# A squared-ReLU transformer block on one core: another order for the first four blocks, the last pair of blocks and the last token tiles

## Chip, core and metric

The kernel runs on one core of one Trainium2 chip. Its time is the device time of one execution in microseconds (us); of several runs the median is given. The engines are named as the profile names them: PE (TensorE, matmul), PEld (its weight loads), DVE (VectorE), ACT (ScalarE), POOL (GpSimd) and SP (SyncE, which issues loads and stores here). Each engine works through its own instructions in the order in which the program lists them.

## What is computed

One layer on a sequence of 1024 tokens with 1024 features: a mixer, then an MLP. Only the MLP is touched:

```python
h = rms_norm(x, norm2_pre) * (1.0 + scale2) + shift2
f = jnp.square(jax.nn.relu(h @ w_fc1)) @ w_fc2      # 1024 -> 4096 -> 1024
x = x + gate2 * rms_norm(f, norm2_post)
```

## The kernel before

Every fp32 product is made of three passes: each operand is split into a high part (a cast by ACT) and a low part (a subtraction by DVE), and PE multiplies high by high, low by high and high by low.

**First product of the MLP, `expand()`.** Both matrices are cut into quarters, and seven products of sums of quarters (a Strassen scheme, numbered 1 to 7) take the place of eight. The 4096 columns of `w_fc1` are worked in 16 blocks n = 0 to 15 (`FP`). A product m of block n is `run(m, n)`: 12 matmuls (4 k-steps by 3 passes) of 128x512. Products 1, 6, 5 and 3 of a block add up in one PSUM bank (`alpha`, tiles a0 to a15), products 7 and 4 in a second (`pi`, p0 to p15), product 2 in a third (`beta`, b0 to b15). After some of them the running sum has to be taken out of the bank before the next product adds to it; that is `after(m, n)`: a copy by ACT after 1, 7 and 6, an add by DVE after 2, 4 and 5, and after 3 a copy, a Relu and a Square by ACT. A block's results lie in a tile F with three parts, and the pool of F tiles (`hx`) has two buffers, so block n takes the buffer of block n - 2 when that has been read. `block_sums(n)` is four DVE instructions that make five sums (tiles S and S3, one buffer each) out of F and c11 (the result of products 1 and 2), stored to DRAM by POOL; c11 of the first four blocks has by then been stored and is loaded again (`again(n)`, tiles c11r). The weights of a block come as two tiles (wa, wo); `T1`, `T32`, `T4` are DVE subtractions that make sums of their quarters, `hi_of` and `lo_of` make the high and low parts that PE reads (hia and loa for products 1 and 2, hic and loc for 7 and 6, hib and lob for 4 and 5; `b22` and `b22_lo` make bhi and blo for product 3).

For the first four blocks all these calls are written out by hand, line by line (lines 882 to 1031), since the token side of the second half is made ready at the same time; from block 4 on a loop repeats one pattern (lines 1032 to 1078). Blocks 2 and 3 run side by side, with products 1 and 2 of block 4 between their last ones. In the loop a block's products come as 7, 6, 4, then 1 of the next block, 5, then 2 of the next block, 3. The last block has no next one, so its five products 7, 6, 4, 5, 3 follow each other, with the calls that make ready the first steps of the next product (`second.fill`).

**Second product, `contract()`.** Seven products again (order 5, 3, 7, 4, 2, 1, 6), each 8 steps of 24 matmuls over four token tiles. In the last product the last two steps are done tile by tile, so that a tile is complete after its 12 last matmuls and goes through `done(6, i, ...)`: `more_of` (DVE adds the bank to acc), `weigh` (ACT squares and sums, DVE updates the mean square and hands it to POOL's power function, DVE multiplies by the gate G), and `finish` (two DVE instructions that scale and add the residual, and two stores on SP). `finish` needs POOL's result.

Of the kernel before, what the change touches and what calls it, by code (L numbers as in the profile page):

```python
# [8 lines left out]
F32 = mybir.dt.float32  # L9
# [7 lines left out]
P = 128  # L17
# [23 lines left out]
def block_kernel(  # L41
# [6 lines left out]
    nc = tc.nc  # L48
# [3 lines left out]
    NT = HT // P  # L52
# [532 lines left out]
    def load_a(n):  # L585
        wa[n] = load_cols(2 * n * P, f"wa{n}")

    def load_o(n):
        wo[n] = load_cols((2 * n + 1) * P, f"wo{n}")
# [6 lines left out]
    def hi_of(kind, n):  # L596
        src = {"a": wa, "c": wo, "b": wa}[kind][n]
        nc.scalar.copy(unit_tiles(kind, n)[0], src)  # L598

    def lo_of(kind, n):  # L600
        src = {"a": wa, "c": wo, "b": wa}[kind][n]
        hi, lo = unit[kind, n]
        nc.vector.tensor_tensor(lo, src, hi.bitcast(F32), ALU.subtract)  # L603

    def b22(n):
        unit["d", n] = (where[n // 2 % 2].tile([P, KH, P], F32R, tag="bhi", name=f"bhi{n}"),
                        where[n // 2 % 2].tile([P, KH, P], F32R, tag="blo", name=f"blo{n}"))
        nc.scalar.copy(unit["d", n][0], wo[n][:, KH:KT])

    def b22_lo(n):  # L610
        hi, lo = unit["d", n]
        nc.vector.tensor_tensor(lo, wo[n][:, KH:KT], hi.bitcast(F32), ALU.subtract)
# [5 lines left out]
    def T1(n):  # L618
        b11, b21, b12, b22 = parts(n)
        sub(b11, b12, b11)  # L620

    def T32(n):
        b11, b21, b12, b22 = parts(n)
        sub(b12, b22, b12)
        sub(b22, b22, b11)

    def T4(n):
        b11, b21, b12, b22 = parts(n)
        sub(b21, b21, b22)
# [96 lines left out]
    NF = 4  # L726
    FP = DFF // (2 * P)
# [4 lines left out]
    fD = [dram.tile([P, 2, 7, 512], F32, name=f"fD{kk}") for kk in range(FK)]  # L732
    F_A11, F_A22, F_S = 0, 1, 2
# [14 lines left out]
    def expand():  # L748
# [9 lines left out]
        hx = stage_pool("hx", 2)  # L758
# [73 lines left out]
        alpha, beta, pi, c11s, F = {}, {}, {}, {}, {}  # L832

        def run(m, n):
            bank = {2: beta, 4: pi, 7: pi}.get(m, alpha)
            if m in (1, 2, 7):
                bank[n] = ps_tile(f"{'abp'[(1, 2, 7).index(m)]}{n}")
            product(bank[n], m, n, m in (1, 2, 7))


        def after(m, n):
            if m == 1:
                c11s[n] = c11p.tile([P, 512], F32, tag="c11", name=f"c11_{n}")
                nc.scalar.copy(c11s[n], alpha[n])
            elif m == 2:
                c = add(c11s[n], beta[n], c11s[n])
                nc.vector.scalar_tensor_tensor(c, c, 0.0, c, ALU.max, ALU.mult)
                nc.gpsimd.dma_start(out=fD[n // 2][:, n % 2, F_A11], in_=c)
            elif m == 7:
                F[n] = hx.tile([P, 3, 512], F32, tag="F", name=f"F{n}")  # L850
                nc.scalar.copy(F[n][:, 0], pi[n])  # L851
            elif m == 6:
                nc.scalar.copy(F[n][:, 1], alpha[n])
            elif m == 4:
                add(F[n][:, 1], pi[n], F[n][:, 1])
            elif m == 5:
                add(F[n][:, 0], alpha[n], F[n][:, 0])
            else:
                nc.scalar.copy(F[n][:, 2], alpha[n])  # L859
                nc.scalar.activation(F[n], F[n], AF.Relu)  # L860
                nc.scalar.activation(F[n], F[n], AF.Square)  # L861
                nc.gpsimd.dma_start(out=fD[n // 2][:, n % 2, F_A22], in_=F[n][:, 0])

        def again(n):
            c11s[n] = c11p.tile([P, 512], F32, tag="c11", name=f"c11r_{n}")
            nc.sync.dma_start(out=c11s[n], in_=fD[n // 2][:, n % 2, F_A11])

        def block_sums(n):
            t, c = F[n], c11s[n]
            at = fD[n // 2][:, n % 2]  # L870
            s = late["fsum"].tile([P, 2, 512], F32, tag="S", name=f"S{n}")
            cb = c.rearrange("p (o n) -> p o n", o=1).broadcast_to([P, 2, 512])
            add(s, cb, t[:, 0:3:2])
            nc.gpsimd.dma_start(out=at[:, F_S:F_S + 2], in_=s)
            s = late["fsum"].tile([P, 3, 512], F32, tag="S3", name=f"S3_{n}")
            add(s[:, 0], t[:, 1], t[:, 0])
            sub(s[:, 1], t[:, 1], c)
            sub(s[:, 2], t[:, 2], t[:, 0])
            nc.gpsimd.dma_start(out=at[:, F_S + 2:], in_=s)
# [49 lines left out]
        T4(0)  # L929
        hi_of("b", 0)  # L930
        run(7, 0)
        after(2, 2)
        after(7, 0)
        his("A22")
        lo_of("b", 0)
# [3 lines left out]
        T4(1)  # L939
        hi_of("b", 1)  # L940
        run(6, 0)
        after(2, 3)
        after(6, 0)
        his("S1")
        lo_of("b", 1)
# [5 lines left out]
        again(0)  # L951
        load_a(3)
        load_o(3)
        again(1)
        run(4, 0)
        last_sums()
        after(4, 0)
# [12 lines left out]
        hi_of("c", 2)  # L970
        run(3, 0)
        after(5, 1)
        T1(3)
        b22_lo(3)
        lo_of("c", 2)
        T32(3)
        T4(2)
        run(3, 1)
        hi_of("c", 3)
        after(3, 0)  # L980
        hi_of("b", 2)
        lo_of("c", 3)
        after(3, 1)
        run(7, 2)
        block_sums(0)
        T4(3)
        lo_of("b", 2)
        after(7, 2)
        run(7, 3)
        hi_of("b", 3)  # L990
        load_a(4)
        run(6, 2)
        block_sums(1)
        lo_of("b", 3)
        after(6, 2)
        after(7, 3)
        again(2)
        load_o(4)
        load_a(5)
        run(6, 3)  # L1000
        hi_of("a", 4)
        after(6, 3)
        lo_of("a", 4)
        b22(4)
        run(4, 2)
        T1(4)
        run(5, 2)
        after(4, 2)
        b22_lo(4)
        run(4, 3)  # L1010
        after(5, 2)
        T32(4)
        hi_of("c", 4)
        run(3, 2)
        after(4, 3)
        T4(4)
        lo_of("c", 4)
        run(1, 4)
        after(3, 2)
        hi_of("b", 4)  # L1020
        run(5, 3)
        after(1, 4)
        again(3)
        lo_of("b", 4)
        hi_of("a", 5)
        run(2, 4)
        block_sums(2)
        after(5, 3)
        run(3, 3)
        lo_of("a", 5)  # L1030
        after(2, 4)
        for n in range(NF, FP):
            more = n + 1 < FP
            if more:
                load_o(n + 1)
                if n + 2 < FP:
                    load_a(n + 2)

            if more:
                b22(n + 1)  # L1040
            after(3, n - 1)
            if more:
                T1(n + 1)
                b22_lo(n + 1)
            else:
                second.fill(1)
            run(7, n)
            after(7, n)
            block_sums(n - 1)
            run(6, n)  # L1050
            after(6, n)
            if more:
                T32(n + 1)
                hi_of("c", n + 1)
            else:
                second.fill(2)
            run(4, n)
            after(4, n)
            if more:
                lo_of("c", n + 1)  # L1060
                T4(n + 1)
                hi_of("b", n + 1)
                run(1, n + 1)
                after(1, n + 1)
                lo_of("b", n + 1)
            run(5, n)
            after(5, n)
            if more:
                if n + 2 < FP:
                    hi_of("a", n + 2)  # L1070
                    lo_of("a", n + 2)
                run(2, n + 1)
                after(2, n + 1)
            else:
                second.fill(3)
            run(3, n)
        after(3, FP - 1)
        block_sums(FP - 1)
        st.close()
# [54 lines left out]
    def contract():  # L1134
# [44 lines left out]
        def more_of(c, i, ps, op=ALU.add):  # L1179
            nc.vector.tensor_tensor(at(c, i), at(c, i), ps, op)  # L1180

        def done(m, i, ps):
            if m == 5:
                put(11, i, ps, -1.0)
                put(12, i, ps)
            elif m == 3:
                put(22, i, ps)
                more_of(12, i, ps)
                weigh(i, 1, True)
            elif m == 7:  # L1190
                more_of(11, i, ps)
            elif m == 4:
                put(21, i, ps)
                more_of(11, i, ps)
            elif m == 2:
                more_of(21, i, ps)
                more_of(22, i, ps, ALU.subtract)
                weigh(NT + i, 0, True)
            elif m == 1:
                more_of(11, i, ps)  # L1200
                more_of(22, i, ps)
                weigh(i, 0, False)
                finish(i)
                fetch_x(NT + i, nc.gpsimd)
            else:
                more_of(22, i, ps)
                weigh(NT + i, 1, False)
                finish(NT + i)


        def gate_row(kt):
# [488 lines left out]
```

## Time and profile before

| | |
|---|---|
| median of 3 runs | 934.15 us (932.95 to 935.11) |
| the profiled execution's own time | 935.21 us |
| its span, first to last instruction | 933.5 us |
| PE busy | 892.4 us (96%), 3960 matmuls |
| DVE, ACT, POOL busy | 686.9 us (74%), 418.8 us (45%), 88.6 us (9%) |
| mean granted clock of TensorE | 0.989 of full speed |

A row of a timeline gives start and duration of an instruction in us, engine, line, operation and tiles, and in brackets the idle time of its engine just before it with what ended that. Matmuls overlap: each row lasts about 0.39 us, but they start some 0.23 us apart.

### The profile page before, as it was taken

The page shows a single profiled execution, that of the slowest core. Times are in us where ns is not written, and L with a number is a line of the kernel's source. Part 1 is how long each engine was busy: PE and PEld are TensorE (multiplying, and loading weights), DVE is VectorE, ACT ScalarE, POOL GpSimd, SP SyncE. Part 2 cuts the span into 40 slices and gives each one's busy share as a digit, 9 for nine tenths or more (in the row PEclk, how much of TensorE's full clock was granted, in tenths as well). Part 3 has the DMA queues.
Part 4 walks back from the last instruction along what each step waited for, and adds up shares of the span by engine and source line. Part 5 has one row for each costly group of instructions (what it writes and reads, how often), then busy time and mean ns, then how long its engine had stood idle before and what let it go on. Part 6 is the DMA issues. An engine that isn't in the chain of part 4 may idle for free.

```text
span 933.5 us, 10776 instructions
## 1 busy us (share of the span) xinstructions
PE 892.4 (96%) x3960; PEld 726.0 (78%) x3960; DVE 686.9 (74%) x980; ACT 418.8 (45%) x558; POOL 88.6 (9%) x147
## 2 busy tenths in 40 slices
PE   4999999999999997999999999999999999999993
PEld 3788678888887786788888888778888888888882
DVE  6889888799658984765666656567987774669694
ACT  3323674235367563445444354444445433434431
POOL 4001020012002000111110111100000000000032
PEclk9999999999999998999999999999999999999997
DMA  9934256575724336543444434489976884334753
GB/s 310 354 104 148 89 158 194 169 250 201 224 68 146 101 100 217 193 146 136 146 169 148 145 136 150 164 311 389 345 237 200 278 274 129 91 115 140 241 181 135
DMA packets 114105, 173.52 MB, mean 186 GB/s; under 512 B 6098, under 2 KB 61442, under 8 KB 114052
## 3 DMA queue, kind: packets, MB, share of 16 engines
q1 hardware_dynamic: 104292, 135.03, 45.0%
q0 software_dynamic: 9760, 37.80, 10.7%
q8 instruction: 31, 0.51, 0.2%
q14 instruction: 22, 0.18, 0.1%
HBM read 135.06 MB, written 37.75 MB: 185 GB/s over the span
## 4 chain that ended last, share of the span: by engine, by line
PE 49%; issue 34%; DVE 8%; ACT 4%; DMA 2%; POOL 1%; SPq 0%; POOLq 0%; DVEq 0%; ACTq 0%
PE a L828 5%; PE a L829 5%; PE a L830 5%; PE pb L1411 3%; PE p L828 2%; PE po L85 2%; PE p L830 2%; PE p L829 2%; PE pu L1586 2%; PE po L86 2%; PE po L87 2%; PE pv L85 2%; PE pv L87 2%; PE pv L86 2%; PE b L829 1%
## 5 line engine op out<-in xcount | busy, mean ns | idle before, releaser
L85 PE MATMUL m<-thi,shi 128*128 128x512 f32 x448 | 174.5, 390 | 0.0
L86 PE MATMUL m<-tlo,shi 128*128 128x512 f32 x448 | 174.5, 390 | 0.0
L87 PE MATMUL m<-thi,slo 128*128 128x512 f32 x448 | 174.5, 390 | 0.0
L94 DVE TENSOR_TENSOR slo<-s,shi 128x1024 fp32r<-128x1024 f32 x56 | 68.4, 1222 | 53.0 <-ACT shi L91 53.0
L91 ACT CAST shi<-s 128x1024 fp32r<-128x1024 f32 x56 | 58.9, 1052 | 102.7 <-PE m L86 61.2
L87 PEld LDWEIGHTS m<-thi,slo 128*128 128x128 f32 x448 | 84.2, 188 | 17.5
L86 PEld LDWEIGHTS m<-tlo,shi 128*128 128x128 f32 x448 | 84.2, 188 | 17.4
L85 PEld LDWEIGHTS m<-thi,shi 128*128 128x128 f32 x448 | 84.2, 188 | 17.3
L91 ACT CAST thi<-wt 128x1024 fp32r<-128x1024 f32 x40 | 42.1, 1052 | 42.1 <-DVE wt L571 34.5
L91 ACT CAST whi<-w_raw 128x1024 fp32r<-128x1024 f32 x28 | 29.3, 1052 | 52.6 <-DMA w_raw<-in_w_in_dram 15.2
L571 DVE TENSOR_TENSOR wt<-wt,b 128x1024 f32<-128x1024 f32 x32 | 39.1, 1222 | 17.4 <-DMA b<-in_w_fc_dram 15.8
L94 DVE TENSOR_TENSOR tlo<-wt,thi 128x1024 fp32r<-128x1024 f32 x40 | 48.9, 1223 | 2.2 <-ACT thi L91 0.8
L571 DVE TENSOR_TENSOR S<-c,F 128x1024 f32<-128x1024 f32 x12 | 14.7, 1225 | 42.4 <-ACT F L861 42.4
L94 DVE TENSOR_TENSOR wlo<-w_raw,whi 128x1024 fp32r<-128x1024 f32 x28 | 34.1, 1220 | 6.2 <-ACT whi L91 6.2
L859 ACT COPY F<-a 128x512 f32<-128x512 f32 x16 | 9.4, 585 | 59.4 <-PE a L830 59.4
L291 POOL TENSOR_TENSOR f<-msf,neg_half 128x1 f32<-128x1 f32 x8 | 7.2, 901 | 286.7 <-DVE msf L1153 286.7
L598 ACT CAST hic<-wo 128x1024 fp32r<-128x1024 f32 x16 | 16.8, 1052 | 35.3 <-DVE wo L571 35.3
L828 PE MATMUL p<-hA,hib 128*128 128x512 f32 x64 | 26.6, 416 | 5.9 <-ACT F L851 5.2
L603 DVE TENSOR_TENSOR lob<-wa,hib 128x1024 fp32r<-128x1024 f32 x16 | 19.6, 1224 | 16.9 <-ACT hib L598 16.9
L181 DVE SCALAR_TENSOR_TENSOR ada_acc<-ada_raw,silu_c,ada_acc 128x1024 f32<-128x1024 f32 x21 | 26.9, 1281 | 4.1 <-DMA ada_raw<-in_w_ada_dram 4.0
L598 ACT CAST hib<-wa 128x1024 fp32r<-128x1024 f32 x16 | 16.8, 1048 | 29.3 <-DVE wa L571 29.3
L828 PE MATMUL a<-hS,bhi 128*128 128x512 f32 x64 | 25.4, 397 | 2.7 <-DVE F L571 2.7
(311 smaller groups left out, 2200.1 us busy)
## 6 DMA issues: line engine op xcount, KB each, us to landing
s<-fD SPq DMA_DIRECT2D x56, 512.0 KB, 4.3
wt<-in_w_fc_dram SPq DMA_DIRECT2D x40, 512.0 KB, 5.2
ada_raw<-in_w_ada_dram SPq DMA_DIRECT2D x24, 512.0 KB, 4.5
fD<-S POOLq DMA_DIRECT2D x16, 768.0 KB, 4.0
wa<-in_w_fc_dram SPq DMA_DIRECT2D x20, 512.0 KB, 4.0
piece<-in_w_ada_dram SPq DMA_DIRECT2D x16, 512.0 KB, 8.3
w_raw<-in_w_out_dram SPq DMA_DIRECT2D x16, 512.0 KB, 4.4
wo<-in_w_fc_dram SPq DMA_DIRECT2D x16, 512.0 KB, 4.4
```

The costliest lines, as they stand in the source:

```text
L85: nc.tensor.matmul(ps, lhsT=ah, rhs=bh, start=start, stop=False)
L86: nc.tensor.matmul(ps, lhsT=ah, rhs=bl, start=False, stop=False)
L87: nc.tensor.matmul(ps, lhsT=al, rhs=bh, start=False, stop=stop)
L91: nc.scalar.copy(hi, src)
L94: nc.vector.tensor_tensor(lo, src, hi.bitcast(F32), ALU.subtract)
L181: nc.vector.scalar_tensor_tensor(acc, t, silu_c[:, kt:kt + 1], acc, ALU.mult, ALU.add)
L571: nc.vector.tensor_tensor(o, a, b, op)
L598: nc.scalar.copy(unit_tiles(kind, n)[0], src)
L828: nc.tensor.matmul(ps, lhsT=ah, rhs=bh, start=first, stop=False, skip_group_check=not start)
L829: nc.tensor.matmul(ps, lhsT=ah, rhs=bl, start=False, stop=False, skip_group_check=not start)
L830: nc.tensor.matmul(ps, lhsT=al, rhs=bh, start=False, stop=last, skip_group_check=not start)
L1411: nc.tensor.matmul(pbs[j], lhsT=w[:, j * P:(j + 1) * P], rhs=a, start=k == 0 and n == 0, stop=k == KT - 1 and n == 2)
```

## The change

The last call of `done` (line 1206 on): `finish` of a tile is called after the add of the following tile. The evictions `after(7, n)` and `after(6, n)` can come in either order; the store of F's first part becomes a function of its own, called by `block_sums` except for block 1. The calls of the first four blocks are written in another order, of which the diff shows the parts that the text speaks of. The last block is taken out of the loop and its products run as 6, 7, 5, 4, 3.

```diff
-            elif m == 7:
-                F[n] = hx.tile([P, 3, 512], F32, tag="F", name=f"F{n}")
-                nc.scalar.copy(F[n][:, 0], pi[n])
-            elif m == 6:
-                nc.scalar.copy(F[n][:, 1], alpha[n])
+            elif m in (6, 7):
+                if n not in F:
+                    F[n] = hx.tile([P, 3, 512], F32, tag="F", name=f"F{n}")
+                nc.scalar.copy(F[n][:, 7 - m], (alpha if m == 6 else pi)[n])
...
-                nc.gpsimd.dma_start(out=fD[n // 2][:, n % 2, F_A22], in_=F[n][:, 0])
+
+        def store_22(n):
+            nc.gpsimd.dma_start(out=fD[n // 2][:, n % 2, F_A22], in_=F[n][:, 0])
...
         def block_sums(n):
             t, c = F[n], c11s[n]
+            if n != 1:
+                store_22(n)
...
         run(7, 0)
-        after(2, 2)
         after(7, 0)
...
         hi_of("c", 2)
         run(3, 0)
         after(5, 1)
+        after(3, 0)
+        lo_of("c", 2)
         T1(3)
...
         run(3, 1)
         hi_of("c", 3)
-        after(3, 0)
         hi_of("b", 2)
+        after(3, 1)
+        block_sums(0)
         lo_of("c", 3)
-        after(3, 1)
+        lo_of("b", 2)
         run(7, 2)
-        block_sums(0)
+        load_a(4)
+        store_22(1)
+        after(7, 2)
+        after(2, 2)
...
-                second.fill(3)
             run(3, n)
+
+        n = FP - 1
+        after(3, n - 1)
+        run(6, n)
+        second.fill(1)
+        run(7, n)
+        after(6, n)
+        block_sums(n - 1)
+        run(5, n)
+        after(7, n)
+        second.fill(2)
+        run(4, n)
+        after(5, n)
+        second.fill(3)
+        run(3, n)
+        after(4, n)
         after(3, FP - 1)
         block_sums(FP - 1)
...
                 more_of(22, i, ps)
+                if i:
+                    finish(NT + i - 1)
                 weigh(NT + i, 1, False)
-                finish(NT + i)
+                if i == NT - 1:
+                    finish(NT + i)
```

On DVE, where block 0's sums are made, the order before (the number behind a letter of a name is the block; the number behind the underscore only counts tiles):

```order
L571 TENSOR_TENSOR wo3_3001<-wo3_3001,wa3_2999 128x512
L571 TENSOR_TENSOR wa2_2993<-wa2_2993,wo2_2995 128x512
L603 TENSOR_TENSOR loc3_3123<-wo3_3001,hic3_3122 128x1024
L571 TENSOR_TENSOR S0_3150<-c11r_0_2997,F0_2917 128x1024
L571 TENSOR_TENSOR S3_0_3153<-F0_2917 128x512
L571 TENSOR_TENSOR S3_0_3153<-F0_2917,c11r_0_2997 128x512
L571 TENSOR_TENSOR S3_0_3153<-F0_2917 128x512
L571 TENSOR_TENSOR wa3_2999<-wa3_2999,wo3_3001 128x512
L603 TENSOR_TENSOR lob2_3130<-wa2_2993,hib2_3129 128x1024
L571 TENSOR_TENSOR S1_3192<-c11r_1_3003,F1_2945 128x1024
```

and in the changed kernel:

```order
L571 TENSOR_TENSOR wa2_2987<-wa2_2987,wo2_2989 128x512
L571 TENSOR_TENSOR S0_3127<-c11r_0_2991,F0_2914 128x1024
L571 TENSOR_TENSOR S3_0_3130<-F0_2914 128x512
L571 TENSOR_TENSOR S3_0_3130<-F0_2914,c11r_0_2991 128x512
L571 TENSOR_TENSOR S3_0_3130<-F0_2914 128x512
L603 TENSOR_TENSOR loc3_3118<-wo3_2995,hic3_3117 128x1024
L603 TENSOR_TENSOR lob2_3121<-wa2_2987,hib2_3120 128x1024
L571 TENSOR_TENSOR c11_2_2834<-b2_2836,c11_2_2834 128x512
L847 SCALAR_TENSOR_TENSOR c11_2_2834<-c11_2_2834 128x512
L571 TENSOR_TENSOR wa3_2993<-wa3_2993,wo3_2995 128x512
```

The sums of block 0 now stand ahead of the low part loc3, and the two c11 results of blocks 2 and 3 lie between the sums of blocks 0 and 1.

On PE, the end of blocks 2 and 3, the first matmul of each product (hA22 is product 4, hS1 product 5, hS4 product 3, hb0_0 product 1, hb0_4 product 2), before:

```order
L828 MATMUL p2_3137<-hA22_0_2919,hib2_3129 128x512
...
L828 MATMUL a2_2810<-hS1_0_2967,hib2_3129 128x512
...
L828 MATMUL p3_3162<-hA22_0_2919,hib3_3175 128x512
...
L828 MATMUL a2_2810<-hS4_0_3021,bhi2_3052 128x512
...
L828 MATMUL a4_3290<-hb0_0_2369,hia4_3222 128x512
...
L828 MATMUL a3_2861<-hS1_0_2967,hib3_3175 128x512
...
L828 MATMUL b4_3330<-hb0_4_2409,hia4_3222 128x512
...
L828 MATMUL a3_2861<-hS4_0_3021,bhi3_3055 128x512
```

and in the changed kernel:

```order
L828 MATMUL p2_3137<-hA22_0_2916,hib2_3120 128x512
...
L828 MATMUL a2_2810<-hS1_0_2961,hib2_3120 128x512
...
L828 MATMUL a4_3262<-hb0_0_2369,hia4_3210 128x512
...
L828 MATMUL a2_2810<-hS4_0_3013,bhi2_3044 128x512
...
L828 MATMUL p3_3162<-hA22_0_2916,hib3_3159 128x512
...
L828 MATMUL a3_2861<-hS1_0_2961,hib3_3159 128x512
...
L828 MATMUL b4_3326<-hb0_4_2409,hia4_3210 128x512
...
L828 MATMUL a3_2861<-hS4_0_3013,bhi3_3047 128x512
```

Product 4 of block 3 comes two products later, behind product 1 of block 4 and product 3 of block 2.

On DVE at the end of the program (acc4 to acc7 are the four last token tiles, m6 the last product's banks), before:

```order
L1180 TENSOR_TENSOR acc4_4972<-acc4_4972,m6_0_6881 128x512
L1153 TENSOR_SCALAR msf_4977<-ssf_4976,msf_4977 128x1
L1156 TENSOR_TENSOR acc4_4972<-acc4_4972,G1_5068 128x512
L1166 SCALAR_TENSOR_TENSOR acc4_4972<-acc4_4972,f_4_7166,xb4_6947 128x512 x2
L1180 TENSOR_TENSOR acc5_4973<-acc5_4973,m6_1_6882 128x512
```

and in the changed kernel:

```order
L1187 TENSOR_TENSOR acc4_4972<-acc4_4972,m6_0_6881 128x512
L1160 TENSOR_SCALAR msf_4977<-ssf_4976,msf_4977 128x1
L1163 TENSOR_TENSOR acc4_4972<-acc4_4972,G1_5068 128x512
L1187 TENSOR_TENSOR acc5_4973<-acc5_4973,m6_1_6882 128x512
L1173 SCALAR_TENSOR_TENSOR acc4_4972<-acc4_4972,f_4_7166,xb4_6947 128x512 x2
```

The two instructions of `finish` stand behind the next tile's add.

## Rows read from the trace of the kernel before

**Rows 1.** The page's part 1: busy time, share of the span, instructions.

```profile
PE 892.4 (96%) x3960; PEld 726.0 (78%) x3960; DVE 686.9 (74%) x980; ACT 418.8 (45%) x558; POOL 88.6 (9%) x147
```

**Rows 2.** The waits of PE, whole span: us in total, times, longest us.

```profile
PE p L828 <- ACT F L851: 5.2, 2, 4.7
PE a L828 <- DVE F L571: 2.7, 2, 1.5
...
PE p L828 <- ACT hib L598: 0.7, 1, 0.7
PE p L830 <- DVE lob L603: 0.6, 1, 0.6
```

**Rows 3.** Timeline of PE, 334 to 382 us: start, duration, instruction, idle before.

```profile
334.02 0.39 PE L828 MATMUL a<-hS,bhi 128*128 128x512 f32 x1
...
342.74 0.40 PE L830 MATMUL p<-hS,loc 128*128 128x512 f32 x1
...
361.18 0.79 PE L828 MATMUL p<-hA,hib 128*128 128x512 f32 x1 [4.75 <-ACT F L851]
...
366.47 0.52 PE L828 MATMUL a<-hS,bhi 128*128 128x512 f32 x1
...
381.88 0.39 PE L828 MATMUL p<-hS,hic 128*128 128x512 f32 x1
```

**Rows 4.** Timeline of ACT, 340 to 361 us.

```profile
340.33 0.58 ACT L859 COPY F<-a 128x512 f32<-128x512 f32 x1
...
360.55 0.58 ACT L851 COPY F<-p 128x512 f32<-128x512 f32 x1 [10.23 <-DVE S L571]
```

**Rows 5.** Timeline of DVE, 340 to 361 us.

```profile
340.46 1.22 DVE L603 TENSOR_TENSOR loc<-wo,hic 128x1024 fp32r<-128x1024 f32 x1 [0.52 <-ACT hic L598]
343.98 1.23 DVE L571 TENSOR_TENSOR S<-c11r,F 128x1024 f32<-128x1024 f32 x1 [2.30 <-ACT F L861]
...
346.93 0.68 DVE L571 TENSOR_TENSOR wa<-wa,wo 128x512 f32<-128x512 f32 x1
...
356.61 1.23 DVE L571 TENSOR_TENSOR S<-c11r,F 128x1024 f32<-128x1024 f32 x1 [7.86 <-DMA fD<-S]
...
360.38 1.22 DVE L603 TENSOR_TENSOR lob<-wa,hib 128x1024 fp32r<-128x1024 f32 x1
```

**Rows 6.** Stretches of 1 us: length, busy (x) per engine, PEclk, DMA, GB/s.

```profile
365.00:366.00 1.00, 1.00 (x3) 0.75 (x3) 1.00 (x3) 0.00 (x0) 0.00 (x0) 0.50 0.99 298
...
378.00:379.00 1.00, 0.02 (x1) 0.02 (x1) 1.00 (x3) 0.00 (x0) 0.38 (x1) 1.00 1.18 388
```

**Rows 7.** Issues of DMAs, 319 to 350 us: KB each, us to landing.

```profile
c11r<-fD SPq DMA_DIRECT2D x1, 256.0 KB, 5.2
...
fD<-S POOLq DMA_DIRECT2D x1, 768.0 KB, 8.7
```

**Rows 8.** Timelines of PE and DVE in the last block, 601 to 610 us.

```profile
601.82 0.50 PE L828 MATMUL p<-hA,hib 128*128 128x512 f32 x1 [0.48 <-ACT F L851]
...
609.20 0.50 PE L828 MATMUL a<-hS,bhi 128*128 128x512 f32 x1 [1.52 <-DVE F L571]
...
607.86 0.68 DVE L571 TENSOR_TENSOR F<-p,F 128x512 f32<-128x512 f32 x1
608.46 0.68 DVE L571 TENSOR_TENSOR F<-a,F 128x512 f32<-128x512 f32 x1
```

**Rows 9.** Timelines of PE and DVE at the end, 910 to 926 us.

```profile
917.44 0.39 PE L87 MATMUL m<-thi,slo 128*128 128x512 f32 x1
...
910.08 0.68 DVE L1180 TENSOR_TENSOR acc<-acc,m 128x512 f32<-128x512 f32 x1
...
911.74 0.68 DVE L1156 TENSOR_TENSOR acc<-acc,G 128x512 f32<-128x512 f32 x1
912.88 1.41 DVE L1166 SCALAR_TENSOR_TENSOR acc<-acc,f,xb 128x512 f32<-128x512 f32 x2 [0.46 <-POOL f L291]
...
925.23 1.42 DVE L1166 SCALAR_TENSOR_TENSOR acc<-acc,f,xb 128x512 f32<-128x512 f32 x2 [0.44 <-POOL f L291]
```

More of the change, by code (lines that the diff above doesn't have):

```diff
@@ L941, in expand @@
         run(6, 0)
-        after(2, 3)
         after(6, 0)
@@ L953, in expand @@
         load_o(3)
-        again(1)
         run(4, 0)
@@ L972, in expand @@
         after(5, 1)
+        after(3, 0)
+        lo_of("c", 2)
         T1(3)
         b22_lo(3)
-        lo_of("c", 2)
         T32(3)
@@ L979, in expand @@
         hi_of("c", 3)
-        after(3, 0)
         hi_of("b", 2)
+        after(3, 1)
+        block_sums(0)
         lo_of("c", 3)
-        after(3, 1)
+        lo_of("b", 2)
         run(7, 2)
-        block_sums(0)
+        load_a(4)
+        store_22(1)
+        after(7, 2)
+        after(2, 2)
         T4(3)
-        lo_of("b", 2)
-        after(7, 2)
+        hi_of("b", 3)
         run(7, 3)
-        hi_of("b", 3)
-        load_a(4)
+        after(2, 3)
+        again(1)
+        lo_of("b", 3)
         run(6, 2)
-        block_sums(1)
-        lo_of("b", 3)
         after(6, 2)
-        after(7, 3)
-        again(2)
         load_o(4)
@@ L1001, in expand @@
         hi_of("a", 4)
+        block_sums(1)
+        after(7, 3)
+        again(2)
+        lo_of("a", 4)
         after(6, 3)
-        lo_of("a", 4)
         b22(4)
@@ L1006, in expand @@
         T1(4)
+        b22_lo(4)
         run(5, 2)
         after(4, 2)
-        b22_lo(4)
-        run(4, 3)
-        after(5, 2)
         T32(4)
         hi_of("c", 4)
+        run(1, 4)
+        after(5, 2)
+        lo_of("c", 4)
+        T4(4)
         run(3, 2)
-        after(4, 3)
[L1016 to L1022, printed above, removed]
+        after(1, 4)
+        hi_of("b", 4)
+        run(4, 3)
+        after(3, 2)
+        lo_of("b", 4)
+        run(5, 3)
+        after(4, 3)
         again(3)
-        lo_of("b", 4)
+        run(2, 4)
+        after(5, 3)
         hi_of("a", 5)
-        run(2, 4)
         block_sums(2)
-        after(5, 3)
         run(3, 3)
+        after(2, 4)
         lo_of("a", 5)
[L1031 to L1040, printed above, removed]
-            after(3, n - 1)
[L1042 to L1046, printed above, removed]
+        for n in range(NF, FP - 1):
+            load_o(n + 1)
+            if n + 2 < FP:
+                load_a(n + 2)
+            b22(n + 1)
+            after(3, n - 1)
+            T1(n + 1)
+            b22_lo(n + 1)
             run(7, n)
@@ L1051, in expand @@
             after(6, n)
[L1052 to L1056, printed above, removed]
+            T32(n + 1)
+            hi_of("c", n + 1)
             run(4, n)
             after(4, n)
[L1059 to L1065, printed above, removed]
+            lo_of("c", n + 1)
+            T4(n + 1)
+            hi_of("b", n + 1)
+            run(1, n + 1)
+            after(1, n + 1)
+            lo_of("b", n + 1)
             run(5, n)
             after(5, n)
[L1068 to L1074, printed above, removed]
-                second.fill(3)
-            run(3, n)
+            if n + 2 < FP:
+                hi_of("a", n + 2)
+                lo_of("a", n + 2)
+            run(2, n + 1)
+            after(2, n + 1)
+            run(3, n)
+        n = FP - 1
[13 more added lines that the diff above has]
+        after(4, n)
         after(3, FP - 1)
```

## The prediction, made before the changed kernel ran

> **What bounds the kernel now.** I read the page's first part, then the list of PE's waits, then the timelines of the engines around the longest of those waits. PE is busy 892.4 us, 96% of the span [rows 1], so a new order can gain only where PE waits, plus what follows PE's last matmul. The list of waits names few places in the lines that the change touches: 5.2 us in two waits for ACT's copy into F, 2.7 us in two for DVE's add into F, 0.7 and 0.6 us for weights of block 1 [rows 2]. The timelines place them. The long one, 4.75 us, is product 4 of block 3 at 361.18 us [rows 3]; 0.48 and 1.52 us are products 4 and 3 of block 15 [rows 8]; the other 1.2 us (2.7 less 1.5) is product 3 of block 3, just before 379 us. The end is another kind: PE's last matmul starts at 917.44 and is done 0.39 later, yet DVE starts the last tile's finish at 925.23 [rows 9].
>
> Why 4.75 us: product 4 of block 3 adds to a bank that ACT must first copy into F. That copy had kept ACT idle for 10.23 us, until 360.55 [rows 4], because the buffer was block 1's F and DVE had not yet read it. DVE in turn had waited 7.86 us at 356.61 for the store of block 0's sums, since S has one buffer [rows 5]. That wait has a second price: in the stretch from 365 us PE runs at half its clock, granted 0.50 (1.2 GHz), while after the 1.2 us wait the granted clock stays 1.00 [rows 6]. The product after the long wait took 361.18 to 366.47, 5.3 us instead of some 2.75.
>
> **The four blocks.** Between 334.02 (start of product 3 of block 0) and 342.74 lie 38 matmul starts [rows 3], 0.2295 us each, so a product of 12 takes 2.75 us. From 334.02 to 381.88, the start of block 4's product 7, both orders run the same 14 products: 38.6 us without waits, 47.9 us now. The 9.3 us between them are the 4.75 us, the slow product's 2.5, the 1.2 and slow restarts.
>
> In the new order product 4 of block 3 comes 8.25 us after block 2's product 4 ends, not 2.75. So PE asks for block 1's F late. What does the new order make late instead? On DVE the low part loc3, which the third matmul of block 3's product 7 needs, now stands behind block 0's sums. These need the Square of block 0's F, for which ACT's copy now comes as soon as product 3 of block 0 ends: 334.02 + 2.75 + 0.15 (a matmul's 0.39 less the step) = 336.95. From that copy to the sums it takes 3.65 (340.33 to 343.98), the four sums take 2.95 (343.98 to 346.93) and loc3 1.22 [rows 4, 5]: 336.95 + 3.65 + 2.95 + 1.22 = 344.8. Product 7 wants it at 342.74 [rows 3]. **A new wait of 2.05 us.**
>
> Is anything late after that? DVE: loc3 and lob2 end at 345.9; the four c11 instructions of blocks 2 and 3 (0.65 each), T4 and lob3 bring it to 350.3. Only then come block 1's sums. They need the reload of c11, which SP issues when block 0's sums are read (343.6) and which took at most 5.2 us [rows 7], so 348.8; and the store of block 0's three sums, issued at 343.9. A store of that size took 8.7 us at the worst [rows 7], so 352.6. Then the sums end by 354.5, ACT copies block 3's p into F, and loa4 (1.2 us) is ready by 355.7; product 1 of block 4, the ninth product, wants it at 334.02 + 8 x 2.75 + 2.05 + 0.45 = 358.5. Covered by 2.8 us. Product 4 of block 3 is three products later. The add that product 3 of block 3 waited for now lies a product earlier (product 2 of block 4 runs between and DVE has no sums ahead of it), so the 1.2 us go. The stores that moved on POOL (block 1's F after block 0's sums, two c11 stores after that) wait for nothing later than 349 and nobody waits for them before 353. SP's load of wa4 moves ahead of the c11 reload; ACT casts wa4 only near 350, so neither is late.
>
> So 38.6 + 2.05 = 40.7 against 47.9: **7.2 us**. The waits of 0.7 and 0.6 us in block 1 [rows 2] end with an ACT cast and a DVE subtraction that keep their place; four c11 instructions ahead of them go, so 0 to 1.3 us more; I take 0, since the cast has to wait for DVE's T4 as before.
>
> **The last block.** Products 6 and 7 come first, then 5, then 4, then 3. Product 5 now waits for the copy of product 6, and that copy stands on ACT just where the copy of product 7 stood, behind the Square of block 14 and two casts for the next product. So the 0.48 us at 601.82 [rows 8] stay, under another name. Product 3 waits for the add after product 5. Before, this add came second, at 608.46; now it comes first, at 607.86 [rows 8]; the casts' low parts ahead of it are the same four DVE instructions. PE gains **0.6 us** of the 1.5; the bounds are 0 and 2.0 (both waits gone).
>
> **The end.** Now each tile goes alone through add, Square, mean, gate, POOL's power and finish: 12.35 us for three tiles (912.88 to 925.23), 4.1 each [rows 9]. With the finish one behind, DVE has per tile add 0.6, finish 1.4, mean 0.15, gate 0.6: 2.75 us, and POOL's 0.46 us wait falls under the next add. PE delivers a tile every 12 x 0.227 = 2.7 us, the last at 917.83. The last add then starts near 917.95, the finish of tile 2 ends 2.0 later, mean and gate of tile 3 start by 920.1, and its own finish 1.14 after the gate's start (911.74 to 912.88) [rows 9]: 921.25 against 925.23, **4.0 us**. Bounds: 4.5 if the last tile's chain were as free as now, 2.5 if POOL's 0.5 us stayed in each of three tiles.
>
> **Sum.** 7.2 + 0.6 + 4.0 = 11.8 us. The profiled execution took 935.2, so 923.4 in its own terms; it lies 1.06 above the median of 934.15, which gives a median of **922.4**. The unknown terms put together reach from 9.7 less (0.6 and 1.5 missing) to 15.0 less (1.3, 1.4 and 0.5 more), 924.5 to 919.2.
>
> **The rivals.**
> - *The new wait costs the clock.* PE's granted clock held 1.00 after 1.2 us of waiting and fell to 0.50 after 4.75 [rows 6]; 2.05 lies between, nearer to 1.2. If it falls, some 12 matmuls run at half speed once more, 2.5 us: 924.9. I give it 0.17. The Trainium skill, page "TensorE: Matmul & The Clock Gate", section "A second HAM failure mode: psum-queue depth-cycling", says that short idle times between groups of matmuls can be frequent enough to make the clock swing between its two levels. By that rule the time would be the 924.9 of this rival; the trace agrees for the long wait and speaks against it for the short one.
> - *Block 1's sums still come late.* If the store of block 0's sums lands later than 8.7 us after its issue, everything behind moves: past 355.5 the wait returns in product 1 of block 4, and then in product 3 of block 2, us for us. For: 8.7 us was seen under loads of wo4 and wa5, which now run close to it. Against: it starts 6 us earlier than now. A store of 16 us gives a wait of 5, so 927.4. Chance 0.08.
> - *The end does not follow DVE.* If the last stores set the end, or POOL's power stays in the chain, the tail gives 1 to 2 us instead of 4: 925. Against: SP issues each store right behind its finish. Chance 0.07.
> - *Slower.* The only wait that could do it is the same one at block 1's sums, on DVE, with ACT and PE blocked behind it. It decides when the sums start after 355.5 + 11.8 = 367 us, that is 23 us after the store's issue, 2.7 times the longest landing here; with a slow clock behind it, 2.5 us sooner. A start at 370 would give 937. Chance 0.05.
> - *Given back.* The gain in the first product is given back by the second, whose loads come no faster. Against it: PE waits nowhere in the second product [rows 2], and its loads are issued by the instructions that now come earlier. It would leave 4 us of tail, 930; a time within 0.2% (1.9 us, about what a measurement can tell from no change) needs the tail lost too. Chance 0.03.
>
> The forecast has the other 0.60. **Chances:** faster 0.91 (forecast, the first three rivals without a small part), same 0.04, slower 0.05. **Range:** 919.5 to 928: it takes in the forecast's bounds, the clock, the tail and a store of 16 us, and leaves out the rest.
>
> **What would show it.** In the profile after, PE should have one wait of about 2 us for DVE's loc in product 7 of block 3, before its third matmul; no wait of over 0.7 us in product 4 of block 3; one of 0.5 us for ACT in product 5 of block 15 and one of about 0.9 in product 3; the last four tiles 2.7 to 2.8 us apart on DVE. The forecast is wrong if DVE waits for a store ahead of block 1's sums until after 355, if the granted clock falls behind the new wait, or if the last finish starts later than 4 us after PE's end.

## The result, and the profile after

The changed kernel takes **923.61 us** (median of 4 runs, 922.04 to 924.62); the kernel before took 934.36 beside it (4 runs, 932.95 to 935.11). The ratio is 0.9885, with a 95% interval of 0.9867 to 0.9904: 10.7 us less, between 9.0 and 12.4. The forecast of 922.4 is 1.2 us too low; the measured time lies inside the forecast range.

The profiled execution took 922.04 us (span 920.3), which is 13.2 less than the profiled one of before. That is more than the medians give, and the stretches below tell part of why. The page's part 1 of the changed kernel, against [rows 1]:

```profile
PE 889.4 (97%) x3960; PEld 722.9 (79%) x3960; DVE 687.4 (75%) x980; ACT 419.1 (46%) x558; POOL 89.1 (10%) x147
```

The same work, 3.0 us less of PE's time; 2.9 of them lie in the stretch from product 3 of block 0 to product 7 of block 4 (41.95 us busy before, 39.10 now), where the product at half the clock was. The list of PE's waits of the changed kernel, against [rows 2]:

```profile
PE p L830 <- DVE loc L603: 1.9, 1, 1.9
PE a L828 <- DVE F L571: 0.9, 1, 0.9
...
PE p L828 <- ACT hib L598: 0.7, 1, 0.7
...
PE p L830 <- DVE lob L603: 0.5, 1, 0.5
PE a L828 <- ACT F L852: 0.5, 1, 0.5
```

The 5.2 us are down to 0.5, the 2.7 to 0.9, and a wait of 1.9 for loc is new. PE's timeline of the changed kernel places them. The rows are, in order: the first matmul of the first product (`expand()`), product 3 of block 0, product 7 of block 3, product 4 of block 3, product 7 of block 4, products 5 and 3 of block 15, the first product's last matmul and PE's last.

```profile
281.06 0.39 PE L828 MATMUL a<-hb,hia 128*128 128x512 f32 x1
...
332.41 0.39 PE L828 MATMUL a<-hS,bhi 128*128 128x512 f32 x1
...
343.23 0.50 PE L830 MATMUL p<-hS,loc 128*128 128x512 f32 x1 [1.94 <-DVE loc L603]
...
362.37 0.39 PE L828 MATMUL p<-hA,hib 128*128 128x512 f32 x1
...
373.45 0.39 PE L828 MATMUL p<-hS,hic 128*128 128x512 f32 x1
...
593.38 0.50 PE L828 MATMUL a<-hS,hib 128*128 128x512 f32 x1 [0.48 <-ACT F L852]
...
600.16 0.49 PE L828 MATMUL a<-hS,bhi 128*128 128x512 f32 x1 [0.91 <-DVE F L571]
...
602.80 0.40 PE L830 MATMUL a<-hS,blo 128*128 128x512 f32 x1
...
908.43 0.39 PE L87 MATMUL m<-thi,slo 128*128 128x512 f32 x1
```

Product 4 of block 3 starts at 362.37 without the 4.75 us of [rows 3]. ACT and DVE of the changed kernel, against [rows 4, 5]:

```profile
335.34 0.59 ACT L858 COPY F<-a 128x512 f32<-128x512 f32 x1 [0.78 <-PE a L830]
...
351.86 0.59 ACT L852 COPY F<-p 128x512 f32<-128x512 f32 x1 [1.67 <-DMA fD<-F]
```

```profile
339.00 1.23 DVE L571 TENSOR_TENSOR S<-c11r,F 128x1024 f32<-128x1024 f32 x1
...
341.95 1.22 DVE L603 TENSOR_TENSOR loc<-wo,hic 128x1024 fp32r<-128x1024 f32 x1
...
348.62 1.22 DVE L571 TENSOR_TENSOR S<-c11r,F 128x1024 f32<-128x1024 f32 x1
...
351.56 1.22 DVE L603 TENSOR_TENSOR loa<-wa,hia 128x1024 fp32r<-128x1024 f32 x1
```

From ACT's copy to block 0's sums 3.66 us, from the sums to loc 2.95, and PE goes on where loc ends. Block 1's sums (348.62) wait for nothing; [rows 5] had them wait 7.86 us. ACT's copy into block 3's F ends at 352.45, 9.9 us before product 4 of block 3 asks. DVE at the end of the changed kernel, against [rows 9]:

```profile
908.86 0.69 DVE L1187 TENSOR_TENSOR acc<-acc,m 128x512 f32<-128x512 f32 x1
...
910.91 0.68 DVE L1163 TENSOR_TENSOR acc<-acc,G 128x512 f32<-128x512 f32 x1
912.03 1.41 DVE L1173 SCALAR_TENSOR_TENSOR acc<-acc,f,xb 128x512 f32<-128x512 f32 x2 [0.44 <-POOL f L291]
```

The last finish starts 3.60 us after PE's last matmul starts; before it was 925.23 - 917.44 = 7.79.

**Stretches.** The first product's ends before stand in PE's timeline of the kernel before, so:

```profile
282.43 0.39 PE L828 MATMUL a<-hb,hia 128*128 128x512 f32 x1
...
611.81 0.40 PE L830 MATMUL a<-hS,blo 128*128 128x512 f32 x1
```

With such rows of every profiled execution the span falls into pieces: the start of the first product; A, from there to product 3 of block 0; B, to product 7 of block 4; C, to the first product's last matmul; E, from PE's last matmul to the end of the span. The second product lies between C and E and takes 305.40 us in each of them, to 0.01.

| us | start | A | B | C | E |
|---|---|---|---|---|---|
| before | 282.43 | 51.59 | 47.86 | 229.93 | 16.06 |
| changed | 281.06 | 51.35 | 41.04 | 229.35 | 11.87 |
| tail only | 281.79 | 51.60 | 47.37 | 229.96 | 11.84 |
| four blocks only | 281.46 | 51.37 | 41.06 | 229.95 | 16.13 |
| last block only | 282.27 | 51.61 | 47.89 | 229.35 | 16.15 |
| loc3 first | 281.30 | 51.35 | 39.15 | 229.36 | 11.90 |
| old pair end | 281.56 | 51.34 | 44.02 | 229.36 | 11.89 |
| last casts later | 283.00 | 51.36 | 41.05 | 227.55 | 11.90 |
| longer wait | 283.23 | 51.35 | 43.73 | 229.34 | 11.91 |
| loc3 first and casts later | 282.22 | 51.35 | 39.18 | 227.55 | 11.87 |
| changed, again 1 | 283.38 | 51.36 | 41.03 | 229.34 | 11.86 |
| changed, again 2 | 283.04 | 51.34 | 41.06 | 229.33 | 11.89 |
| changed, again 3 | 281.24 | 51.34 | 42.59 | 229.34 | 11.85 |

A, C and E repeat to 0.1 us wherever their calls stand in the same order, so one profile each tells more of a term than the medians do. B in the old order repeats less closely: its three profiles give 47.37, 47.86 and 47.89, with waits of 4.08 (tail only), 4.75 (before) and 4.54 us (last block only) in product 4 of block 3. The start varies by 2.3 us whatever the order behind it: 1.37 of the 13.2 us between the two first profiles are that.

A good part of that spread is the granted clock, which falls in some executions ahead of the first product too, at two places. In four profiles (before, last block only, old pair end, last casts later) it fell between 24 and 30 us, as here before:

```profile
26.00:27.00 1.00, 1.00 (x4) 0.76 (x3) 1.00 (x3) 1.00 (x3) 0.00 (x0) 0.50 1.05 382
```

They take 84.8 to 84.9 us from PE's wait at 23 to 25 us to its wait near 108 us, the other nine 83.3 to 83.8; so 1.2 of the 1.37 us belong to a fall in the profile of before. In three others (longer wait, again 1, again 2) it fell between 108 and 113 us, as here in again 1:

```profile
108.21 0.50 PE L85 MATMUL po<-whi,ybs 128*128 128x512 f32 x1 [0.88 <-ACT yb L419]
```

```profile
110.00:111.00 1.00, 1.00 (x4) 0.81 (x3) 1.00 (x3) 0.40 (x1) 0.00 (x0) 0.50 0.34 129
```

They take 175.2 us from there to the first product, the other ten 173.6 to 173.7: 1.5 us for a fall. The rest of the spread comes for the most part from the first 25 us.

### The profile page after: what moved, and what is told of

Same layout as the page of the kernel before. It is cut to its first block, busy times and chain, and to the rows that moved or that the text cites. A ratio compares the mean times of both kernels' runs of the same rounds, so it can differ in the third digit from the quotient of the medians.

```text
span 920.3 us, 10782 instructions
## 1 busy us (share of the span) xinstructions
PE 889.4 (97%) x3960; PEld 722.9 (79%) x3960; DVE 687.4 (75%) x980; ACT 419.1 (46%) x558; POOL 89.1 (10%) x147
## 4 chain that ended last, share of the span: by engine, by line
PE 53%; issue 32%; DVE 8%; ACT 4%; DMA 2%; POOL 1%; SPq 0%; POOLq 0%; DVEq 0%; ACTq 0%
PE a L828 6%; PE a L829 6%; PE a L830 6%; PE p L830 3%; PE p L829 3%; PE p L828 3%; PE pb L1421 3%; PE po L85 2%; PE pu L1596 2%; PE po L86 2%; PE po L87 2%; PE pv L85 2%; PE pv L87 2%; PE pv L86 2%; PE b L828 1%
## 5 line engine op out<-in xcount | busy, mean ns | idle before, releaser
L85 PE MATMUL po<-whi,ybs 128*128 128x512 f32 x64 | 25.8, 406 | 1.6 <-ACT yb L419 0.9
L830 PE MATMUL p<-hS,loc 128*128 128x512 f32 x64 | 25.4, 397 | 1.9 <-DVE loc L603 1.9
```

Source lines behind the costliest of these rows:

```text
L85: nc.tensor.matmul(ps, lhsT=ah, rhs=bh, start=start, stop=False)
L830: nc.tensor.matmul(ps, lhsT=al, rhs=bh, start=False, stop=last, skip_group_check=not start)
```

## The experiments

**The three parts alone.** Each is the kernel before with one part of the change. The tail:

```diff
                 more_of(22, i, ps)
+                if i:
+                    finish(NT + i - 1)
                 weigh(NT + i, 1, False)
-                finish(NT + i)
+                if i == NT - 1:
+                    finish(NT + i)
```

> The kernel before with only the finish of the last four tiles one behind. Theory (the forecast's term for the tail): the last finish starts 4.0 us sooner, so the time is 934.4 - 4.0 = 930.4 us, and nothing in the first product moves (PE still waits 4.7 us for ACT's copy into F). Rival (the end does not follow DVE): 1 to 2 us less, 932.4 to 933.4.

Measured: 930.15 us against 934.53, ratio 0.9952 (0.9938 to 0.9967), 4.4 us less. In its trace, PE's last matmul and DVE's last finish:

```profile
916.36 0.39 PE L87 MATMUL m<-thi,slo 128*128 128x512 f32 x1
```

```profile
919.96 1.42 DVE L1166 SCALAR_TENSOR_TENSOR acc<-acc,f,xb 128x512 f32<-128x512 f32 x2 [0.44 <-POOL f L291]
```

3.60 us between them, as in the changed kernel, and E is 4.2 us shorter: the end follows DVE, and the rival falls. The wait for ACT's copy was 4.08 us instead of the 4.7 expected, and B 0.5 us shorter than before, though no line there changed; that is the spread of B noted above.

The four blocks; of the edit the core:

```diff
         hi_of("b", 2)
-        lo_of("c", 3)
         after(3, 1)
-        run(7, 2)
         block_sums(0)
-        T4(3)
+        lo_of("c", 3)
         lo_of("b", 2)
+        run(7, 2)
...
         after(4, 2)
-        b22_lo(4)
-        run(4, 3)
...
+        run(4, 3)
+        after(3, 2)
```

> The changed order of the first four blocks alone, with the last block and the tail as before. Theory: 7.2 us less than before, 927.2 us; in the profile the waits of 4.7 and about 1.2 us are gone, PE waits about 2 us for DVE's loc in product 7 of block 3, the granted clock behind that wait stays 1.00, and the waits of 0.5 (ACT F) and 1.5 us (DVE F) of the last block are as before. Rival (given back by the second product): under 2 us less.

Measured: 928.78 us, ratio 0.9943 (0.9926 to 0.9959), 5.7 us less; the interval, 3.8 to 6.9, ends just short of 7.2. In the profile A and B are 7.0 us shorter together, and the second product gives nothing back. PE's waits in its timeline:

```profile
343.67 0.50 PE L830 MATMUL p<-hS,loc 128*128 128x512 f32 x1 [1.94 <-DVE loc L603]
...
601.21 0.51 PE L828 MATMUL a<-hS,bhi 128*128 128x512 f32 x1 [1.51 <-DVE F L571]
```

The new wait is there and the last block's 1.5 us stand as before. The profile agrees with the theory. The median gains 1.3 us less than the 7.0; the runs on the clock below show what can add 1.5 us to an execution, but whether it did in these runs is not shown, since only one of them has a profile.

The last block:

```diff
+        run(6, n)
+        second.fill(1)
+        run(7, n)
+        after(6, n)
+        block_sums(n - 1)
+        run(5, n)
+        after(7, n)
...
```

> The kernel before with only the order 6, 7, 5, 4, 3 in the last block. Theory: 0.6 us less, 933.8 us, which the runs can hardly tell from nothing; the profile can: one wait of 0.5 us for ACT's F in product 5 and one of 0.9 us for DVE's F in product 3, in place of 0.5 and 1.5 us. Rival (nothing gained): the two waits sum to 2.0 us as before.

Measured: 934.29 us, ratio 0.9995 (0.9986 to 1.0005), which the runs can't tell from nothing. The profile can: C is 0.58 us shorter, by these rows of PE against [rows 8]:

```profile
601.71 0.50 PE L828 MATMUL a<-hS,hib 128*128 128x512 f32 x1 [0.49 <-ACT F L852]
...
608.49 0.50 PE L828 MATMUL a<-hS,bhi 128*128 128x512 f32 x1 [0.93 <-DVE F L571]
```

**Is the new wait only the order on DVE?** The changed kernel with one call moved:

```diff
+        lo_of("c", 3)
         block_sums(0)
-        lo_of("c", 3)
         lo_of("b", 2)
```

> The changed kernel with one call moved: the low part loc3 ahead of the sums of block 0 on DVE. Theory (PE's wait of 1.9 us is only the order on DVE, and the sums have room): the wait is gone, the sums of block 0 come not over 1.2 us later, and nothing behind them is late, so 2.0 us less than the changed kernel: 923.6 - 2.0 = 921.6 us. Rival (the sums have no room): the wait comes back in product 1 of block 4 or in the products after it, and the time is that of the changed kernel, 923.6 us.

Measured: 920.98 us, ratio to before 0.9855 (0.9841 to 0.987), where the changed kernel has 0.9885. B is 1.89 us shorter. In its DVE timeline loc3, the sums of blocks 0 and 1, and loa4:

```profile
340.18 1.23 DVE L603 TENSOR_TENSOR loc<-wo,hic 128x1024 fp32r<-128x1024 f32 x1 [0.98 <-ACT hic L598]
341.32 1.22 DVE L571 TENSOR_TENSOR S<-c11r,F 128x1024 f32<-128x1024 f32 x1
...
349.79 1.22 DVE L571 TENSOR_TENSOR S<-c11r,F 128x1024 f32<-128x1024 f32 x1
...
352.73 1.22 DVE L603 TENSOR_TENSOR loa<-wa,hia 128x1024 fp32r<-128x1024 f32 x1
```

Block 0's sums come 2.1 us later than with the change (2.3 by these rows, of which 0.24 is the later start), more than the 1.2 expected, since loc3 has to wait 0.98 us for its cast. Block 1's come 0.9 later, and loa4 is ready 1.1 us before product 1 of block 4 starts at 355.09. The expected 1.2 was too small, but the sums had the room, and A, C and E are as in the changed kernel: the change's new wait can be avoided at no cost elsewhere.

**What removed the 4.75 us, the earlier sums or PE's order?** The changed kernel with the pair's end in the old order:

```diff
         run(5, 2)
         after(4, 2)
+        b22_lo(4)
+        run(4, 3)
+        after(5, 2)
...
-        run(1, 4)
-        after(5, 2)
...
-        run(4, 3)
-        after(3, 2)
```

> The changed kernel, but from product 4 of block 2 up to the loop the calls stand in the old order: product 4 of block 3 again comes right behind product 5 of block 2, two products sooner than in the change. Theory (the earlier sums on DVE removed the 4.75 us wait): ACT's copy into block 3's F ends at 352.4 us on the changed kernel's axis and product 4 of block 3 asks at 356.9, so it doesn't wait; only the wait of about 1.2 us for DVE's add ahead of product 3 of block 3 comes back: 923.6 + 1.2 = 924.8 us. Rival (the later product 4 is what removed the wait): PE waits 3 us or more there, with half the clock behind it, 927 us or more.

Measured: 925.29 us, ratio 0.9897 (0.9881 to 0.9914). Its rows of PE (product 7 of block 3, product 4 of block 3, product 3 of block 3) and of ACT:

```profile
343.73 0.50 PE L830 MATMUL p<-hS,loc 128*128 128x512 f32 x1 [1.94 <-DVE loc L603]
...
358.90 0.40 PE L828 MATMUL p<-hA,hib 128*128 128x512 f32 x1
...
374.06 0.50 PE L828 MATMUL a<-hS,bhi 128*128 128x512 f32 x1 [1.17 <-DVE F L571]
```

```profile
352.23 0.59 ACT L852 COPY F<-p 128x512 f32<-128x512 f32 x1
```

Product 4 of block 3 does not wait though it comes in its old place: ACT's copy ends 6 us ahead of it. So PE's new order is not what removed the long wait; it is worth the 1.17 us before product 3 of block 3, as the theory has it. B is 3.0 us longer here, not 1.2: some 0.2 by which the matmuls next to a wait run apart, and the rest is the clock. The same view of stretches as in [rows 6], for this kernel:

```profile
344.00:345.00 1.00, 1.00 (x6) 0.78 (x5) 1.00 (x2) 1.00 (x2) 0.00 (x0) 1.00 1.07 434
...
346.00:347.00 1.00, 1.00 (x4) 0.75 (x3) 1.00 (x3) 0.22 (x1) 0.54 (x1) 0.50 1.01 422
```

Behind the same wait of 1.94 us the granted clock falls to 0.50 (1.2 GHz), which it didn't in the changed kernel's profile:

```profile
345.00:346.00 1.00, 1.00 (x6) 0.82 (x5) 1.00 (x2) 0.00 (x0) 0.28 (x2) 1.00 1.06 432
```

PE's new order with block 0's sums in their old place was not run. By the rows of before it would only have moved the wait: product 1 of block 4 would have come at about 356.4, and its weights' high part was not ready until 362.1, since its cast stands behind the late copy on ACT:

```profile
361.03 1.05 ACT L598 CAST hia<-wa 128x1024 fp32r<-128x1024 f32 x1
```

"Earlier sums" hides a second move. What block 1's sums waited for was the store of block 0's (S has one buffer), and POOL issues the stores in the order of its calls. Before, the store of block 1's F stood ahead of it and waited 3.93 us for that block's Square; so the store of S went out at 349.24, though the sum was ready at 345.21:

```profile
348.71 0.54 POOL L862 DMA_DIRECT2D fD<-F  x1 [3.93 <-ACT F L861]
349.24 0.54 POOL L874 DMA_DIRECT2D fD<-S  x1
```

The change puts that store of F (`store_22(1)`) behind block 0's sums. In the changed kernel and with loc3 first the store of S goes out 0.3 us after its sum:

```profile
340.52 0.54 POOL L877 DMA_DIRECT2D fD<-S  x1 [0.72 <-DVE S L571]
```

```profile
342.83 0.54 POOL L877 DMA_DIRECT2D fD<-S  x1 [2.79 <-DVE S L571]
```

Counted from product 3 of block 0, block 0's sums start 3.4 us sooner in the changed kernel, its store 7.1 us sooner. With loc3 first the sums start only 1.3 us sooner than before and the store 5.0, and block 1's sums wait for nothing even so. In both kernels, then, 3.7 us of the earlier store are the order on POOL. No run has one of the two moves without the other, so how much of the 4.75 us each removes, and whether either alone would have been enough, is open.

**The clock.** First a longer wait, the changed kernel with

```diff
-        lo_of("c", 3)
         lo_of("b", 2)
+        lo_of("c", 3)
```

> The changed kernel with the low part lob2 (1.22 us on DVE) ahead of loc3, so that PE's wait in product 7 of block 3 grows from 1.94 to about 3.2 us. Theory (the clock falls only after a longer wait, such as the 4.75 us before): the granted clock behind it stays 1.00 and the kernel takes 1.2 us more, 924.8 us. Rival (a wait between 2 and 4.75 us is enough): the granted clock falls to 0.50 behind it, 2.5 us on top, 927.3 us.

Measured: 925.97 us, ratio 0.9908 (0.9894 to 0.9923). PE's row and a stretch behind it:

```profile
346.55 0.50 PE L830 MATMUL p<-hS,loc 128*128 128x512 f32 x1 [3.07 <-DVE loc L603]
```

```profile
348.00:349.00 1.00, 1.00 (x4) 0.81 (x3) 1.00 (x2) 0.55 (x1) 0.54 (x1) 0.50 1.01 400
```

The wait is 1.13 us longer and the clock falls; B is 2.7 us longer, so the fall costs 2.7 - 1.1 = 1.6, not 2.5. The theory of this run, that it takes a longer wait to cost the clock, is wrong.

Then the changed kernel three times more, unaltered:

> The changed kernel once more, unaltered, to see whether the granted clock behind its 1.94 us wait is the same in every execution: behind the same wait it stayed 1.00 in the changed kernel's profile, and fell to 0.50 where the pair's end had the old order. Theory (the same wait costs the clock in some executions and not in others): the first product takes 321.7 us from its first matmul to its last where the clock holds and some 1.5 us more, 323.2, where it falls; of three executions at least one falls. Rival (it holds in this kernel, and the spread of its times is from the stretch ahead of the first product): 321.7 us in all three.

> As the run before it: 321.7 us with the clock at 1.00 behind the wait, or 323.2 with a stretch at 0.50.

> As the two runs before it: 321.7 us with the clock at 1.00 behind the wait, or 323.2 with a stretch at 0.50.

Measured: 924.31, 923.98 and 923.72 us. The wait is 1.94 in all three. A stretch behind it in the first and in the third:

```profile
347.00:348.00 1.00, 1.00 (x5) 0.77 (x5) 0.96 (x3) 0.21 (x1) 0.55 (x1) 1.00 1.12 453
```

```profile
345.00:346.00 1.00, 1.00 (x3) 0.77 (x3) 0.97 (x3) 0.03 (x1) 0.40 (x1) 0.50 1.10 447
```

The clock fell in one of three, and the first product took 321.73, 321.73 and 323.27 us: 1.54 for a fall. The theory holds: the clock can fall behind this wait. The rival holds a part, since the start of the first product, 281.24 to 283.38, moves the time too; but 1.5 of these 2.1 us are again the clock, which fell near 108 us in the first two of the three executions. Each of the three thus had one such fall, at one place or the other. Over all seven profiled executions with a wait of 1.94 us (these three, the changed kernel's first, four blocks only, old pair end, last casts later) it fell in two.

**The last block's waits, and both moves.** The changed kernel with the casts for the second product behind the evictions:

```diff
         run(6, n)
-        second.fill(1)
         run(7, n)
         after(6, n)
+        second.fill(1)
         block_sums(n - 1)
         run(5, n)
         after(7, n)
-        second.fill(2)
         run(4, n)
         after(5, n)
+        second.fill(2)
         second.fill(3)
```

> The changed kernel with the casts for the second product moved behind the evictions in the last block: the first group of casts behind the copy of product 6, the second behind the add after product 5. Theory (both waits are only the order on ACT and DVE): the waits of 0.5 (ACT F, product 5) and 0.9 us (DVE F, product 3) are gone and the second product starts without a wait, so 1.4 us less, 922.2 us. Rival (the casts come too late): the second product's first matmuls wait for a cast or its low part, and the time is that of the changed kernel or above it.

Measured: 921.83 us, ratio 0.9864 (0.985 to 0.9879). C is 1.8 us shorter: the two waits, 1.4, and 0.4 by which the matmuls next to a wait run apart. The second product starts 0.24 us after the first one's last matmul, as it does everywhere, so the casts aren't late, and the rival falls.

> The changed kernel with both moves: loc3 ahead of block 0's sums, and the casts of the last block behind the evictions. Theory (the gains lie in different stretches and add up): 1.9 us less in the first four blocks as with the first move alone, 1.4 us less in the last block, 923.6 - 3.3 = 920.3 us. Rival (the second move gains nothing): the time of the first move alone, 921.0 us to 921.7 us.

This one has both edits, as shown above. Measured: **919.87 us**, ratio 0.9842 (0.9827 to 0.9856), 14.5 us less than before, and its interval lies clear of the changed kernel's. B and C are those of the two moves alone, so the gains add up. Of the waits in the lines that the change touches its list keeps two:

```profile
PE p L828 <- ACT hib L598: 0.7, 1, 0.7
...
PE p L830 <- DVE lob L603: 0.5, 1, 0.5
```

## Why the prediction was right, point by point

- **The new wait** (forecast 2.05 us): 1.94. The chain was followed right: copy to sums 3.65 forecast and 3.66 measured, the sums 2.95 and 2.95, then loc3.
- **The four blocks** (forecast 7.2 us): A and B together 7.06, where the clock held. B fell by 6.82; the 38.6 us without waits were 0.5 too low, since without the new wait it is still 39.15 (loc3 first). A gave 0.24: the waits in block 1 that I took as unchanged (0 to 1.3) became a little shorter. That the sum comes within 0.15 us is in part luck: the two misses have opposite signs, and B before varied by 0.5 us between profiles.
- **Why 4.75 us.** The chain of the prediction (DVE waits for the store of block 0's sums, ACT for DVE, PE for ACT) is what the rows show, but it leaves out that 4.0 us of the store's lateness were its place behind another store on POOL. The prediction named the move of that store only as harmless.
- **Cover behind it.** Forecast: block 1's sums end by 354.5 and loa4 2.8 us ahead of its product. On the changed profile's axis, which lies 1.6 us earlier, the 354.5 is 352.9. Measured: the sums end at 351.64 and loa4 4.1 us ahead (352.78 against 356.86), since DVE waited neither for a store nor for a reload; ahead of the product's third matmul, which the forecast reckoned with, it is 4.5. Product 4 of block 3 comes two products after that one, not three as the prediction says; with its 9.9 us of room nothing rested on it. The rival that has block 1's sums late is wrong, and so is the slower one, which needed the same wait.
- **The last block** (forecast 0.6 us): 0.58, with the waits under the names foretold.
- **The end** (forecast 4.0 us): 4.19. On DVE the adds of the last three tiles start 2.72 us apart, as foretold (2.7 to 2.8), and only the last tile still waits for POOL (0.44).
- **The sum**: 7.06 + 0.58 + 4.19 = 11.8, as forecast, for an execution in which the clock holds. With the B of the other two profiles in the old order it is 11.3 and 11.9. The medians give 10.7 (9.0 to 12.4).
- **The rival on the clock** had its chance, 0.17, put as if the clock would fall in every run or in none. It fell in two of seven, one of them an execution of the changed kernel itself (again 3), and for that one the prediction's own sign of being wrong came true. A fall costs 1.5 us, not 2.5: I had taken the whole product of [rows 6] at half speed, but behind the shorter wait the slow stretch is shorter (below 1.00 from 345 to 349 in old pair end; before from 359 to 367, with PE at work from 361.18). The row at 378 us in [rows 6] lies inside the wait of 1.2 us; the stretches behind it, to 382 us, stand at 1.00 too. At 2 of 7 that is 1.54 x 2 / 7 = 0.4 us of a mean time, which brings the 11.8 to 11.4, inside the interval. The rest of the difference from 10.7 is no larger than the runs' spread from the start of the first product, to which the falls ahead of it add 1.2 to 1.5 us in some executions of either kernel; it isn't assigned to any step. Of the two readings that the prediction weighed, that of the Trainium skill (page "TensorE: Matmul & The Clock Gate", section "A second HAM failure mode: psum-queue depth-cycling", short idle times between groups of matmuls, frequent enough to make the clock swing) fits the two falls, the other, that a wait this short leaves the clock alone, the five executions at 1.00. A single wait is not what that section tells of; nearer to it are the falls near 108 us, which came behind waits of 0.33, 0.65 and 0.88 us within 4 us (again 1), but waits of the same size there left the clock at 1.00 in the other ten profiles.
- **Given back** by the second product: wrong, it takes 305.40 us everywhere.

## What to carry to other kernels

When a call is moved up, follow what it pushes down on the same engine to the instruction that first misses its due time: that gave the new wait here to 0.1 us, and loc3 first then showed that one subtraction ahead of the sums avoids it. When several edits could have removed one wait, undo each: here undoing PE's new order brought back only 1.2 us, so the long wait was the sums' and their store's; the order of the sums on DVE and that of the stores on POOL were not undone one by one, and their shares stay open. When an engine waits for a store, look when the store was issued, and not only when its data were ready. Where run-to-run spread hides a term of half a microsecond, compare the same stretch between two named instructions in single profiles.

## What was not expected of the hardware

The granted clock behind an identical wait of 1.94 us is not the same in every execution of one kernel: 1.00 in five profiles and 0.50 in two. In the profiled execution with 3.07 us it fell as well. What decides it was not found. The wait stands at the same matmul in all of them, and its time in the execution does not decide it either: it began at 341.5 and 341.8 us in the two falls, and at 341.3, 341.7 and 343.3 to 343.6 in the others. At the two places ahead of the first product it fell in some executions only, too: behind the wait near 24 us (1.53 to 1.54 us in the falls, 1.29 to 1.55 in the others) the clock fell in four profiles of thirteen, and behind the one of 0.9 us near 108 us in three. Those falls are 1.2 to 1.5 us of the spread by which the first product starts; without them it would still be 1.9, which was not traced further.
